# MLP up-projection of a two-layer decoder trunk: twelve gate column pairs computed from seven block products each

## The chip, the cores and the metric

One core of one Trainium2 chip runs the whole kernel. The metric is the device time of one execution in microseconds (us), lower is better. The engines are called as the profile calls them: PE is the matrix engine (TensorE) and PEld its weight load, DVE the vector engine, ACT the scalar engine, POOL GpSimd, and SP the engine whose queue issues the loads. SBUF is the on-chip working memory, PSUM the memory of eight banks (128 partitions by 512 float32 each) that PE writes its results to.

## What is computed

Two layers over 512 tokens with a width of 1024. Each layer has a mixer (attention with a short convolution in layer 0, gated linear attention in layer 1), then a gated MLP, then an embedding added through a gate. The change lies in the MLP:

```python
def _conv_ffn(h, w_up, conv_w, conv_b, w_down):
    u = _causal_depthwise_conv(h @ w_up, conv_w) + conv_b
    gate, up = jnp.split(u, 2, axis=-1)
    return (jax.nn.gelu(gate, approximate=False) * up) @ w_down

# in each layer:
x = x + _conv_ffn(_rms_norm(x, ffn_norm[i]), ffn_w_up[i], ffn_conv_w[i], ffn_conv_b[i], ffn_w_down[i])
```

`w_up` is 1024 by 5632: 2816 gate columns and 2816 value columns. The convolution runs over three tokens of each column by itself. `_rms_norm` divides a token by the root mean square of its 1024 values and multiplies by a gain.

## The kernel before

All large products are made in float32 from two parts: an operand is split into a high part (a cast to the reduced float `fp32r`, made on ACT) and a low part (the difference, made on DVE), and `mm3` (L153) issues three matmuls, high by high, high by low, low by high. `split` (L96) does this for activations, `cut` (L118) for weights.

**The up-projection** is `ffn` (L770). Activations lie transposed, 128 features by 512 tokens, in eight tiles `xT`. `xg` holds them times the gain and split, as eight pairs in the buffers with the tags a0 and a1, eight of each; the division by the root mean square is not in them. It comes later, as a multiplication by `R` (a tile with each token's factor), in `taps`. The loop over d = 0 to 10, called blocks here, takes 256 gate columns and the 256 value columns that belong to them. A block loads two weight tiles of 1 MB into `raw` (two buffers, SP queue), cuts each into two pairs `wh`, `wl` (three buffers of each), and then computes four columns of 128: gate and value for c = 0, gate and value for c = 1. A column is 8 x 3 = 24 matmuls of 512 tokens that gather in one PSUM bank from `ps` (four banks; `pa` has the other four).

For each column, `taps` multiplies the bank by R into `z` (DVE, L785), scales it and adds the bias (ACT, L786) and adds the two earlier tokens with two fused multiply-adds (DVE, L788). The gate goes through Gelu (ACT, L810), gate and value are multiplied (DVE, L813), and the product is split at once (L101, L102) into its place in `acts`: the first eight of 22 in the buffers b0 and b1, the others in quarters of tiles tagged `four` (seven buffers). `zt`, the tile of tap results, has four buffers of 512 columns.

After the loop, `project` (L349) multiplies `acts` with the down-projection's weights, two output columns at a time, eight products of gate and value (k) at a time, and `done` adds the result to `xT`. In layer 1, `blocks` (L281) there prepares sums of halves for `ple1`, the last stage, which already works from seven products of quarter matrices.

**Order.** Within `manual_schedule` blocks the named engines keep the program's order. Elsewhere the framework's planner sets the order of each engine's instructions when the kernel is built, from estimated costs, the program's order and when buffers come free. Engines run their queues in that order. Two instructions on different engines that touch the same PSUM bank are kept apart.

Of the kernel before, what the change touches and what calls it, by code (L numbers as in the profile page):

```python
# [18 lines left out]
P = 128  # L19
S = 512  # L20
D = 1024
NT = S // P
ND = D // P
DFF = 2816
NF = DFF // P
# [31 lines left out]
class Kernel:  # L57
# [709 lines left out]
            self.end_norm()  # L767


    def ffn(self, i, next_gain):  # L770
        nc, a, tc = self.nc, self.a, self.tc
        xg, R = self.xg, None
        wu = a["ffn_w_up"][i].rearrange("(k p) n -> p k n", p=P)
        w0, w1, w2, bb = self.fcv
        with tc.tile_pool(name=f"ffn{i}", bufs=1) as fp:
            acts = [self.pair(self.fp, "b0", "b1") for f in range(8)]
            for f in range(8, NF, 2):
                four = self.four(fp)
                acts += [(four[:, 0], four[:, 1]), (four[:, 2], four[:, 3])]

            def taps(ps, f):
                y = fp.tile([P, S], F32, tag="zt", name=self.nm("zt"), bufs=4)
                z = fp.tile([P, S + 2], F32, tag="z", name=self.nm("z"), bufs=3)
                nc.gpsimd.memset(z[:, :2], 0.0)
                nc.vector.tensor_tensor(z[:, 2:], ps, R, ALU.mult)  # L785
                nc.scalar.activation(y, z[:, 2:], AF.Identity, scale=w2[:, f : f + 1], bias=bb[:, f : f + 1])  # L786
                for tap, w in ((1, w1), (0, w0)):
                    nc.vector.scalar_tensor_tensor(  # L788
                        out=y, in0=z[:, tap : tap + S], scalar=w[:, f : f + 1], in1=y, op0=ALU.mult, op1=ALU.add
                    )  # L790
                return y

            for d in range(NF // 2):
                wg = self.weights(wu[:, :, 256 * d : 256 * d + 256], ND, 256)
                wv = self.weights(wu[:, :, DFF + 256 * d : DFF + 256 * d + 256], ND, 256)
                for c in range(2):
                    f = 2 * d + c
                    got = []
                    pss = []
                    for w in (wg, wv):  # L800
                        ps = self.ps()
                        for k in range(ND):
                            self.mm3(ps, w(k, c * P, (c + 1) * P), xg[k], start=k == 0, stop=k == ND - 1)
                        pss.append(ps)
                    if R is None:
                        R = self.spread()
                    for w, ps, fo in ((wg, pss[0], f), (wv, pss[1], NF + f)):
                        y = taps(ps, fo)
                        if w is wg:
                            nc.scalar.activation(y, y, AF.Gelu)  # L810
                        got.append(y)
                    g, y = got
                    nc.vector.tensor_tensor(y, g, y, ALU.mult)  # L813
                    self.split(acts[f], y)
            self.begin_norm(("a0", "a1"))
            done = self.residual(next_gain)
            if i == 1:
                self.forms = []
                scratch = lambda: fp.tile([P, S], F32, tag="zt", name=self.nm("gx"), bufs=4)

                def done(m, ps):
                    nc.vector.tensor_tensor(self.xT[m], self.xT[m], ps, ALU.add)
                    self.blocks(m, next_gain, scratch)
# [75 lines left out]
    def ple1(self, fp):  # L899
# [49 lines left out]
        def back(hf, t):  # L949

            pb = self.pa()
            for q in range(4):
                nc.tensor.transpose(
                    pb[:, q * P : (q + 1) * P], self.xT[4 * hf + q][:, t * P : (t + 1) * P], self.ident
                )
            x = fp.tile([P, 512], F32, tag="zt", name=self.nm("xt"), bufs=4)
            nc.scalar.copy(x, pb)
            return x

# [45 lines left out]
        X, Q = [[self.ps() for _ in range(2)] for _ in range(2)]  # L1005
        both = (0, H)
        with tc.manual_schedule(engines={ET.PE, ET.DVE, ET.Activation}):
# [3 lines left out]
            steps = [(j, i, both, Q[i]) for j in range(J) for i in range(2)]  # L1011
# [38 lines left out]
            halves = ((0, H // 2), (H // 2, H))  # L1050
# [482 lines left out]
```

## Time and profile before

| | |
|---|---|
| runs of the kernel before | 1247.49, 1248.13, 1248.69 us; median 1248.13 |
| the profiled execution | 1248.2 us, of it 1246.4 us span from the first to the last instruction |
| clock granted to PE in it | 1.000 |
| bytes moved by DMA | 117.45 MB, mean 94 GB/s |
| up-projection, layer 0 | about 186 to 425 us of the span |
| up-projection, layer 1 | about 828 to 1068 us of the span |

How to read it: a row of the groups names line, engine, operation, output <- inputs, shape and count, then busy us, mean ns of one, and the idle time of the engine just before, with what ended it. A matmul's row gives its length with the drain, which overlaps the next; the spacing of starts in the timeline is what one costs. Fences in the prediction show whole lines of the views, with "..." where lines are left out.

### The profile page before, as it was taken

The numbers are of one execution on the slowest core, as the hardware profiler recorded it, in microseconds if no ns is written. First come the engines' busy times: TensorE is split into PE (matmuls) and PEld (weight loads), VectorE is DVE, ScalarE is ACT, GpSimd is POOL, SyncE is SP. The second block draws the span as 40 slices with busy tenths as digits, with TensorE's granted clock in tenths as the row PEclk, the third lists the DMA queues.
The fourth block names the chain that finished last, engine by engine and source line by source line (L and its number), as shares of the span: only waits on it lengthen the run. The fifth ranks groups of instructions, "written<-read, shape, count | busy, mean of one in ns | idle before, by whom it ended". The sixth has DMA issues, their size and how long they took to land.

```text
span 1246.4 us, 15216 instructions
## 1 busy us (share of the span) xinstructions
PE 1236.1 (99%) x5984; PEld 1023.9 (82%) x5984; DVE 804.6 (65%) x1251; ACT 561.5 (45%) x873; POOL 52.1 (4%) x152
## 2 busy tenths in 40 slices
PE   9999999999999999999999999999999999999998
PEld 8877788888888888888987878888888888888887
DVE  6886556777777633346679875557777777444495
ACT  7466344444444322234563554335444444333374
POOL 2500000000000000000100000000000000000000
PEclk9999999999999999999999999999999999999999
DMA  6222232233333232223322222332223333322411
GB/s 214 92 80 56 83 102 83 88 100 102 101 102 101 83 103 93 93 74 103 111 91 68 69 68 68 101 110 95 83 94 102 101 101 102 101 93 94 149 46 68
DMA packets 111004, 117.45 MB, mean 94 GB/s; under 512 B 2728, under 2 KB 106210, under 8 KB 110932
## 3 DMA queue, kind: packets, MB, share of 16 engines
q1 hardware_dynamic: 109568, 115.35, 28.4%
q8 instruction: 47, 0.77, 0.2%
q0 software_dynamic: 560, 0.42, 0.2%
q10 hardware_dynamic: 804, 0.70, 0.2%
q14 instruction: 25, 0.20, 0.0%
HBM read 114.37 MB, written 2.10 MB: 93 GB/s over the span
## 4 chain that ended last, share of the span: by engine, by line
PE 88%; DVE 7%; ACT 2%; issue 1%; POOL 1%; DVEq 0%; ACTq 0%; POOLq 0%
PE ps L157 26%; PE ps L158 26%; PE ps L159 26%; DVE wl L138 1%; PE ps L947 1%; PE ps L946 1%; PE ps L945 1%; PE pa L1367 1%; PE pa L1344 0%; PE pa L595 0%; PE pa L158 0%; PE pa L192 0%; PE pa L159 0%; DVE F L1228 0%; PE pa L157 0%
## 5 line engine op out<-in xcount | busy, mean ns | idle before, releaser
L137 ACT ACTIVATE wh<-raw 128x1024 fp32r<-128x1024 f32 (+4 forms) x212 | 214.2, 1012 | 333.3 <-PE ps L158 298.7
L138 DVE TENSOR_TENSOR wl<-raw,wh 128x1024 fp32r<-128x1024 f32 (+4 forms) x212 | 246.5, 1164 | 153.2 <-ACT wh L137 152.1
L157 PE MATMUL ps<-a,wh 128*128 128x512 f32 x864 | 336.9, 390 | 0.0
L158 PE MATMUL ps<-a,wh 128*128 128x512 f32 x864 | 336.6, 390 | 0.0
L159 PE MATMUL ps<-a,wl 128*128 128x512 f32 x864 | 336.3, 389 | 0.0
L158 PEld LDWEIGHTS ps<-a,wh 128*128 128x128 f32 x864 | 162.3, 188 | 34.0 <-issue 0.3
L159 PEld LDWEIGHTS ps<-a,wl 128*128 128x128 f32 x864 | 162.2, 188 | 33.9
L157 PEld LDWEIGHTS ps<-a,wh 128*128 128x128 f32 x864 | 162.2, 188 | 33.7 <-issue 0.7
L788 DVE SCALAR_TENSOR_TENSOR zt<-z,vfa,zt 128x512 f32<-128x512 f32 x176 | 131.3, 749 | 3.6 <-ACT zt L786 0.6
L157 PE MATMUL ps<-b,wh 128*128 128x512 f32 x320 | 126.0, 395 | 0.5 <-ACT b L101 0.5
L159 PE MATMUL ps<-b,wl 128*128 128x512 f32 x320 | 125.7, 393 | 0.0
L158 PE MATMUL ps<-b,wh 128*128 128x512 f32 x320 | 125.0, 391 | 0.0
L785 DVE TENSOR_TENSOR z<-ps,R 128x512 f32<-128x512 f32 x88 | 60.3, 687 | 74.7 <-PE ps L159 74.7
L157 PE MATMUL ps<-four,wh 128*128 128x512 f32 x224 | 87.1, 389 | 0.0
L158 PE MATMUL ps<-four,wh 128*128 128x512 f32 x224 | 87.1, 389 | 0.0
L159 PE MATMUL ps<-four,wl 128*128 128x512 f32 x224 | 87.1, 389 | 0.0
L786 ACT ACTIVATE zt<-z,vfb 128x512 f32<-128x512 f32 x88 | 70.9, 808 | 5.0 <-DVE z L785 3.3
L157 PEld LDWEIGHTS ps<-b,wh 128*128 128x128 f32 x320 | 60.0, 188 | 14.0 <-ACT b L101 1.3
L159 PEld LDWEIGHTS ps<-b,wl 128*128 128x128 f32 x320 | 60.1, 188 | 12.5
L158 PEld LDWEIGHTS ps<-b,wh 128*128 128x128 f32 x320 | 60.1, 188 | 12.5
L810 ACT ACTIVATE zt<-zt 128x512 f32<-128x512 f32 x44 | 27.8, 631 | 74.9 <-DVE zt L788 74.8
L101 ACT ACTIVATE four<-zt 128x512 fp32r<-128x512 f32 x28 | 17.7, 632 | 77.3 <-DVE zt L813 77.3
(359 smaller groups left out, 1555.0 us busy)
## 6 DMA issues: line engine op xcount, KB each, us to landing
raw<-in_ffn_w_up_dram SPq DMA_DIRECT2D x44, 1024.0 KB, 5.1
raw<-in_ffn_w_down_dram SPq DMA_DIRECT2D x16, 1024.0 KB, 4.7
raw<-in_hy_w_in_dram SPq DMA_DIRECT2D x8, 1024.0 KB, 5.0
raw<-in_gla_w_in_dram SPq DMA_DIRECT2D x8, 1024.0 KB, 5.3
raw<-in_ffn_w_down_dram SPq DMA_DIRECT2D x8, 768.0 KB, 4.1
raw<-in_ple_w_gate_dram SPq DMA_DIRECT2D x6, 1024.0 KB, 4.7
raw<-in_gla_w_out_dram SPq DMA_DIRECT2D x4, 1024.0 KB, 4.8
raw<-in_gla_w_in_dram SPq DMA_DIRECT2D x4, 672.0 KB, 4.0
```

Source lines behind the costliest of these rows:

```text
L101: nc.scalar.activation(h, src, AF.Copy)
L137: nc.scalar.activation(hv, v, AF.Copy)
L138: nc.vector.tensor_tensor(lv, v, hv.bitcast(F32), ALU.subtract)
L157: mm(out, lh, rh, start=start, stop=False)
L158: mm(out, lh, rl, start=False, stop=False)
L159: mm(out, ll, rh, start=False, stop=stop)
L785: nc.vector.tensor_tensor(z[:, 2:], ps, R, ALU.mult)
L786: nc.scalar.activation(y, z[:, 2:], AF.Identity, scale=w2[:, f : f + 1], bias=bb[:, f : f + 1])
L788: nc.vector.scalar_tensor_tensor(out=y, in0=z[:, tap : tap + S], scalar=w[:, f : f + 1], in1=y, op0=ALU.mult, op1=ALU.add)
L810: nc.scalar.activation(y, y, AF.Gelu)
L945: mm(o, lh, rh, start=first and j == 0, stop=False, **kw)
L946: mm(o, lh, rl, start=False, stop=False, **kw)
```

## The change

For blocks d = 4 to 9 of each layer (`SEVEN`), the two gate columns are computed in another way. Input features, gate columns and tokens are each split in two, which makes the product of two gate columns a product of matrices of 2 by 2 quarters. Instead of eight quarter products, seven are computed (a Strassen-like form), each with 4 x 3 matmuls of 256 tokens. `sums` makes the four sums of token quarters (once a layer, in blocks 0 to 3, as splits in b0 and b1), `seven_forms` the sums of weight quarters, and `seven` issues the products. `W` and `V` are banks of `pa`; `X` and `Y` (banks of `ps`) hold the two results, with 256 tokens in each half. Copies on ACT seed and pass on partial sums; `more`, the product V, is added to `Y` in `taps`. The first value column of a block, `V0`, is computed in two halves between the products, the second, `V1`, behind them (before them in block 4). PE's order is kept by hand in these blocks.

The sums have to be formed from normed activations, so from block 4 on x times gain times R is the operand: `sums` computes it into `scratch`, and at block 4 it is split into eight new a0, a1 pairs. From there `taps` no longer multiplies by R and reads PSUM directly. Products of gate and value stay in float32 in `kept` (tiles tagged `four`), since b0 and b1 are in use; all 22 are split after block 9, the first eight one by one, the others two at a time. `zt` has two buffers of 1024 columns, so that Gelu and the product run over both columns at once. The memsets of two columns of `z` on POOL are gone. In the last stage `half()` hands out halves of the `zt` tiles.

```diff
+SEVEN = (4, 10)
+    def sums(self, j, gain, R, scratch):
...
+        for u in range(2):
+            m = 2 * j + u
+            nc.vector.scalar_tensor_tensor(
+                out=scratch[:, u], in0=self.xT[m], scalar=gain[:, m : m + 1], in1=R, op0=ALU.mult, op1=ALU.mult
+            )
+        e, o, s12, s34 = (scratch[:, u] for u in range(4))
+        out = []
+        nc.vector.tensor_tensor(s12[:, :H], e[:, H:], o[:, H:], ALU.add)
...
+        for x in (s12, s34):
+            hl = self.pair(self.fp, "b0", "b1")
+            self.split(hl, x)
...
+    def seven_forms(self, raw):
...
+        (b11, b12), (b21, b22) = self.blocks_of(raw)
+        plain = self.cut_blocks(raw[:, :, :P])
+        nc.vector.tensor_tensor(b11, b12, b11, ALU.subtract)
+        nc.vector.tensor_tensor(b12, b22, b12, ALU.subtract)
+        t13 = self.cut_blocks(raw.rearrange("p (j u) n -> p j u n", u=2)[:, :, 0])
+        nc.vector.tensor_tensor(b11, b22, b11, ALU.subtract)
+        t2 = self.cut_blocks(b11, False)
+        nc.vector.tensor_tensor(b21, b21, b11, ALU.subtract)
+        return plain, t13, t2
+
+    def seven(self, raw, ws, xg, forms):
...
+        W, V = self.pa(), self.pa()[:, :H]
+        X, Y = self.ps(), self.ps()
...
+        def product(out, w, c, x, first=False):
...
+            for j in range(ND // 2):
+                (wh, wl), (xh, xl) = w(j, c), x(j)
+                mm(out, wh, xh, start=first and j == 0, stop=False, **kw)
+                mm(out, wh, xl, start=False, stop=False, **kw)
+                mm(out, wl, xh, start=False, stop=j == ND // 2 - 1, **kw)
...
+        product(W[:, left], plain, 0, tokens(0, 0), True)
+        nc.scalar.copy(X[:, left], W[:, left])
+        nc.scalar.copy(Y[:, left], W[:, left])
+        product(V, t13, 0, s1, True)
+        more = self.sp.tile([P, S], F32, tag="acc", name=self.nm("more"), bufs=1)[:, :H]
+        nc.scalar.copy(more, V)
+        product(X[:, left], plain, 1, tokens(1, 0))
+        product(Y[:, left], t2, 0, s2)
+        nc.scalar.copy(X[:, right], Y[:, left])
+        yield
+        last = self.cut_blocks(raw.rearrange("p (j u) n -> p j u n", u=2)[:, :, 1])
+        product(X[:, right], t13, 1, s3)
+        nc.scalar.copy(Y[:, right], X[:, right])
+        yield
+        product(Y[:, left], last, 1, s4)
+        product(X[:, right], last, 0, tokens(1, 1))
+        yield X, Y, more
...
     def ffn(self, i, next_gain):
...
+            scratch = [self.four(fp, F32) for _ in range(ND // 2)]
             for d in range(NF // 2):
-                wg = self.weights(wu[:, :, 256 * d : 256 * d + 256], ND, 256)
-                wv = self.weights(wu[:, :, DFF + 256 * d : DFF + 256 * d + 256], ND, 256)
...
-                    self.split(acts[f], y)
+                g, y = both(), both()
+                normed = d >= SEVEN[0]
+                if d == SEVEN[0]:
+                    xg = []
+                    for m in range(ND):
+                        xg.append(self.pair(self.fp, "a0", "a1"))
+                        self.split(xg[m], scratch[m // 2][:, m % 2])
...
+                    with tc.manual_schedule(engines={ET.PE}):
+                        if d == SEVEN[0]:
+                            rg, rv = loaded(d)
+                            V1 = second()
+                            taps(y[:, 1], V1, NF + 2 * d + 1)
+                            ws, w = self.seven_forms(rg), column(rv, 0)
+                        steps = self.seven(rg, ws, xg, forms)
+                        next(steps)
+                        V0 = self.pa()
+                        value(w, V0, 0, ND // 2)
+                        next(steps)
+                        value(w, V0, ND // 2, ND)
+                        X, Y, more = next(steps)
+                        if d > SEVEN[0]:
+                            V1 = second()
+                        if d + 1 < SEVEN[1]:
+                            rg, rv = loaded(d + 1)
+                            ws, w = self.seven_forms(rg), column(rv, 0)
+                        taps(y[:, 0], V0, NF + 2 * d)
+                        taps(g[:, 0], X, 2 * d)
+                        taps(g[:, 1], Y, 2 * d + 1, more)
+                        nc.scalar.activation(g, g, AF.Gelu)
+                        if d > SEVEN[0]:
+                            taps(y[:, 1], V1, NF + 2 * d + 1)
+                else:
...
+                nc.vector.tensor_tensor(u, g, y, ALU.mult)
+                if d < ND // 2:
+                    forms.append(self.sums(d, gain, R, scratch[d]))
+                if d == SEVEN[1] - 1:
+                    for f in range(8):
+                        hl = self.pair(self.fp, "b0", "b1")
+                        self.split(hl, at(f))
+                        acts.append(hl)
+            for d in range(4, NF // 2):
+                split_pair(y if d == NF // 2 - 1 else kept[d // 2][:, 2 * (d % 2) : 2 * (d % 2) + 2])
```

`cut_blocks` casts 1024 weights a partition (512 for t2, in the buffers tagged `sq`) into one pair `wh`, `wl` and returns its quarters; `column` cuts one value column of 1024; `loaded` issues the two loads of a block.

More of the change, by code (lines that the diff above doesn't have):

```diff
@@ L793, in ffn @@
-            for d in range(NF // 2):
-                wg = self.weights(wu[:, :, 256 * d : 256 * d + 256], ND, 256)
-                wv = self.weights(wu[:, :, DFF + 256 * d : DFF + 256 * d + 256], ND, 256)
[L796 to L813, printed above, removed]
-                    self.split(acts[f], y)
+            forms, kept, acts = [], [], []
@@ new lines, in columns, with loaded, column @@
+            def columns(w, c, bank):
+                ps = bank()
+                for k in range(ND):
+                    self.mm3(ps, w(k, c * P, (c + 1) * P), xg[k], start=k == 0, stop=k == ND - 1)
+                return ps
+            def loaded(d):
+                out = [self.raw(ND, 256) for _ in range(2)]
+                for raw, c0 in zip(out, (256 * d, DFF + 256 * d)):
+                    nc.sync.dma_start(raw, wu[:, :, c0 : c0 + 256])
+                return out
+            def column(raw, c):
+                return self.cut(raw[:, :, c * P : (c + 1) * P], "b")
```

112 lines of the change are left out of this document (95 added, 17 removed).

## The prediction

> **What bounds the kernel now.** I read the engines' busy times first, then who the matrix engine (PE) waited for, then the chain that ended last.
>
> ```profile
> PE 1236.1 (99%) x5984; PEld 1023.9 (82%) x5984; DVE 804.6 (65%) x1251; ACT 561.5 (45%) x873; POOL 52.1 (4%) x152
> ...
> PE 88%; DVE 7%; ACT 2%; issue 1%; POOL 1%; DVEq 0%; ACTq 0%; POOLq 0%
> ```
> ```profile
> PE pa L1213 <- DVE F L1211: 1.5, 2, 1.0
> PE pa L1287 <- ACT qT L1279: 1.3, 2, 0.7
> ...
> PE ps L157 <- ACT b L101: 0.5, 1, 0.5
> ```
>
> PE is busy 99% of the span, the chain is 88% PE, and its waits come to some 6 us in all, none of them in the stage that is changed. So time is saved here by fewer PE microseconds or not at all, and whatever makes PE wait is paid in full. Next the stage itself: blocks d = 4 to 9 (the ones that change) of layer 0 and of layer 1, in the view of windows (columns: us, then busy us and instruction count of PE, weight load, DVE, ACT, POOL; clock, DMA share, GB/s).
>
> ```profile
> 272.80:403.30 130.50, 130.50 (x577) 108.09 (x576) 95.47 (x120) 58.92 (x72) 2.39 (x24) 1.00 0.30 97
> 915.50:1046.00 130.50, 130.50 (x577) 108.07 (x576) 95.46 (x120) 58.89 (x72) 2.39 (x24) 1.00 0.30 97
> ```
>
> Six blocks take 130.5 us: 21.75 us each, PE full, DVE 15.9 us (73%), ACT 9.8 us (45%), clock 1.00. A block is 4 columns of 24 matmuls. Two starts of the same place in the pattern, 48 matmuls apart, in the timeline of PE:
>
> ```profile
> 272.78 0.39 PE L157 MATMUL ps<-a,wh 128*128 128x512 f32 x1
> ...
> 283.66 0.39 PE L157 MATMUL ps<-a,wh 128*128 128x512 f32 x1
> ```
>
> (283.66 - 272.78) / 48 = 0.2267 us from start to start for 512 columns; the 0.39 is the length of one with its drain, which overlaps the next.
>
> **What the change removes on PE.** In twelve blocks (six in each layer) the two gate columns, 48 matmuls of 512 columns, become seven products of 12 matmuls, 84 of 256 columns. The price of a 256-column matmul stands in the trace twice, in the last 24 matmuls of the kernel and, in 29 in a row, near its start:
>
> ```profile
> 1239.30 0.28 PE L945 MATMUL ps<-wh,a 128*128 128x256 f32 x1
> ...
> 1242.06 0.28 PE L947 MATMUL ps<-four,b 128*128 128x256 f32 x1
> ```
> ```profile
> 19.75 0.28 PE L158 MATMUL pa<-wl,a 128*128 128x256 f32 x1
> ...
> 23.11 0.28 PE L159 MATMUL pa<-wh,a 128*128 128x256 f32 x1
> ```
>
> 2.76 / 23 and 3.36 / 28 are both 0.120 us, more than half of 0.2267: each matmul carries about 0.013 us that doesn't shrink. So seven eighths of the arithmetic do not give an eighth back: gates before 48 x 0.2267 = 10.88 us, after 84 x 0.120 = 10.08 us. The two value columns stay at 10.88. A block goes from 21.76 to 20.96 us, 0.80 us less, **9.6 us over twelve blocks**. That is all the change can win; nothing else leaves PE. A rule that speaks against it is in the Trainium skill, "TensorE: Matmul & The Clock Gate", section "Back-to-back issue gap": it gives 81 ns for 128 and 131 ns for 512 columns in a stream with weight loads; a straight line between gives an estimate of 98 ns for 256, by which the gates would go from 6.3 to 8.2 us. The trace disagrees with it at 512 columns (227 ns).
>
> **What it adds beside PE.** Durations of the stage, from the groups by shape within the window of blocks 4 to 9, and from other lines a 256-column copy on ACT, a 256-column sum on DVE, the hand-over from PE to ACT and the landing time of a load:
>
> ```profile
> L158 PEld LDWEIGHTS ps<-a,wh 128*128 128x128 f32 x192 | 36.0, 188 | 7.5
> ...
> L788 DVE SCALAR_TENSOR_TENSOR zt<-z,vfa,zt 128x512 f32<-128x512 f32 x48 | 35.9, 749 | 0.8
> L138 DVE TENSOR_TENSOR wl<-raw,wh 128x1024 fp32r<-128x1024 f32 x24 | 29.4, 1225 | 3.0 <-ACT wh L137 2.7
> L137 ACT ACTIVATE wh<-raw 128x1024 fp32r<-128x1024 f32 x24 | 25.5, 1062 | 15.4 <-PE ps L158 15.4
> L786 ACT ACTIVATE zt<-z,vfb 128x512 f32<-128x512 f32 x24 | 19.4, 809 | 0.5
> L785 DVE TENSOR_TENSOR z<-ps,R 128x512 f32<-128x512 f32 x24 | 16.5, 687 | 22.4 <-PE ps L159 22.4
> L813 DVE TENSOR_TENSOR zt<-zt,zt 128x512 f32<-128x512 f32 x12 | 8.3, 692 | 0.4
> L102 DVE TENSOR_TENSOR four<-zt,four 128x512 fp32r<-128x512 f32 x11 | 7.6, 692 | 7.7 <-ACT four L101 7.7
> ...
> L101 ACT ACTIVATE four<-zt 128x512 fp32r<-128x512 f32 x11 | 7.0, 632 | 30.4 <-DVE zt L813 30.4
> ```
> ```profile
> L1351 ACT COPY st<-pa 128x256 f32<-128x256 f32 x4 | 1.5, 375 | 0.0
> ```
> ```profile
> L303 DVE TENSOR_TENSOR gx<-gx,gx 128x256 f32<-128x256 f32 x4 | 1.7, 420 | 0.2 <-ACT gx L288 0.2
> ```
> ```profile
> 1242.37 0.47 ACT L989 ACTIVATE so<-ps,rtok 128x256 f32<-128x256 f32 x1 [0.96 <-PE ps L947]
> ```
> ```profile
> raw<-in_ffn_w_up_dram SPq DMA_DIRECT2D x44, 1024.0 KB, 5.1
> ```
>
> DVE in a block of the seven: five low halves of 1024 (plain, t13, last, two value columns) 5 x 1.22 = 6.1; four weight differences and t2's low half, 5 x 0.69 = 3.5; eight taps 6.0; the sum with `more` 0.69; the product of gate and value in one go, priced as another 128x1024, 1.22. The four multiplications by R and both splits are gone from the block. Sum 17.5 us; the same counting of the old block gives 16.4 where the window shows 15.9 (neighbours overlap a little), so I take 17.0 of 20.96 us, 81%. ACT: casts 5 x 1.06 + 0.63, four scalings 3.2, Gelu about 1.06, five copies of 256 columns 1.9: 12.1 us, 58%. Both stay under PE. Blocks 0 to 3 lose a split (1.4) and gain the token sums (two fused multiplications 1.5, four halves 1.7, two splits 1.4): DVE some 19 of 21.75 us; they depend on nothing of the block and have the whole layer's four blocks to be done in. POOL's memsets go; nobody on the chain waited for them. Bytes moved stay the same, on the same SP queue.
>
> **Where PE could wait inside a block.** Count t from the block's first matmul: products 1 to 4 end at 1.44, 2.88, 4.32, 5.76, the value half at 8.48, product 5 at 9.92, the other half at 12.64, products 6 and 7 at 15.52, the second value column at 20.96. The copies: ACT began 0.03 us after PE's last result above (1242.06 + 0.28 against 1242.37), so the copy of W into X runs from 1.63 to 2.0 and is wanted at 2.88; the copies into the right halves have 2.72 us of value matmuls over them. Cost nothing, cover 0.85 us at the tightest, and 0.2 us each time that a 1.06 us cast stands right in front. The weights: three buffers for five uses. `last` is cut after product 3 and gives the raw buffer back at about 8; the next gate load takes 5.1 us and lands at 13; plain, two differences and t13 are then 1.06 + 1.22 + 0.69 + 0.69 + 1.06 + 1.22, with the hand-overs done at about 19.2, wanted at 22.4. The next value column's buffer comes free at 20.96, it is cut by 23.3, wanted at 26.7. So each chain has some 3.3 us of slack while 6.7 us of taps compete for DVE. I take 0, since the planner that orders DVE and ACT sees those chains first in the program; the other end is 1.9 us a block (below).
>
> **The switch at block 4.** This is the term I am least sure of. The normed x is split into the eight a0/a1 buffers that block 3's last column is still reading: buffer k comes free 24 - 3(k + 1) matmuls before its end, and block 4's first column wants the new pair k 0.68 k us after it. A split takes 0.63 on ACT and 0.69 on DVE, so alone it would be ahead by about 3 us. But DVE has in the same stretch block 3's last taps (0.69 + 1.5, twice), its product 1.22, the cut of the first value column 1.22, and after it plain, t13 and the differences. If the splits go first, 0. If all earlier work goes first, I count 2.9 us until pair 7, 0.5 for plain and 2.2 for t13: 5.6. I take 2.0 a layer, nearer to the low end because plain's buffer is free 10.9 us earlier; **4.0 us for both**.
>
> **The end of the stage.** The splits of all 22 products of gate and value move behind block 9: 8 x 0.69 for the first eight and 7 x 1.22 for the rest, two at a time, 14.1 us of DVE. Block 9 makes no forms for a successor (7 us less) and block 10 needs 12 of its 21.76 us, which leaves some 20 us of room, and the down-projection's first 48 matmuls (10.9 us) read only eight columns. Cost 0; without that cover what is left over would be paid.
>
> **Sum.** From the profiled execution's 1248.2 (span 1246.4): 1248.2 - 9.6 + 4.0 = 1242.6; the runs' median is 0.07 lower, so **1242.5**, its own range 1238.5 (switch free) to 1245.6.
>
> **Rivals.** (1) DVE sets the pace, and the change is slower. Its order is fixed in advance, and in the old block it is idle 21.75 - 15.9 = 5.85 us behind ACT and PE. If the new block keeps that idleness, it lasts 17.0 + 5.85 = 22.85 us: 1.9 us over PE's 20.96, 22.7 us over twelve, 1265; half of it gives 1254. For it: five casts in place of four in the ACT-to-DVE relay, the in-place differences that wait for both halves of t13. Against: much of the old idleness was waiting for PE columns (22.4 us of the window behind L785), which is slack, not need. It decides from 0.47 us of wait a block, (9.6 - 4.0) / 12. (2) The switch costs its upper end: 11.2 - 9.6, 1249.8, no change that can be told (0.2%, 2.5 us, is what a measurement of this kernel can tell). For it: blocks 3 and 4 together ask DVE for about all its time. Against: the splits are ready before the work that competes. (3) The weight load of 188 ns doesn't hide behind a 256-column matmul when every one has new weights: 84 x 0.188 = 15.8, a block 4.9 us longer, 59 us, 1307. Against it: all the 0.120 us matmuls above had their own loads. The Trainium skill's section named above gives its own version of this, an estimate of 1.9 us a block or 1271.
>
> **How the numbers follow.** Forecast 0.60, (1) 0.25, (2) 0.12, (3) 0.03. Faster by over 0.2% is the forecast, 0.60. Within: (2) and the mildest part of (1), 0.13. Slower: the rest of (1) and (3), 0.27. The range runs from 1238, PE's full gain, to 1262; beyond it lie the worst third of (1), (3), and a little below, some 0.15 together.
>
> **What would show it.** Matmuls of 256 columns at 0.120 us start to start, 36 x 12 = 432 more matmuls, and PE busy about 9.6 us less are the gain. The first pairs of block 4 (a0/a1 splits) among what PE waited for, some 2 us in each layer, would be the switch. Waits of PE for wl, wh or a copy that recur with each of the twelve blocks would be rival 1. The forecast is wrong if blocks 5 to 9 take over 21.4 us each, if the 256-column matmuls keep another spacing, or if the first columns of the down-projection wait for b0/b1 splits.

## The result, and the profile after

The changed kernel takes 1258.03 us (median of 6 runs, 1257.71 to 1259.87) against 1247.78 us for the kernel before (6 runs, 1247.06 to 1248.69): a ratio of 1.0084, 95% interval 1.0071 to 1.0097. It is 10.25 us slower where 5.6 us of gain were forecast, and the time lies within the predicted range but on the other side of no change. The profile is that of the execution of 1259.87 us (span 1258.1), 11.7 us above the profiled one of the kernel before.

The page of the changed kernel, engines' busy times and the chain that ended last:

```profile
PE 1235.7 (98%) x6416; PEld 1039.1 (83%) x6416; DVE 850.1 (68%) x1323; ACT 601.2 (48%) x963; POOL 43.6 (3%) x64
...
PE 81%; DVE 12%; ACT 4%; issue 2%; POOL 1%; DMA 0%; ACTq 0%; DVEq 0%; POOLq 0%
```

PE has the 432 more matmuls and is hardly less busy than the 1236.1 us of before; the chain has lost 7 points of PE to DVE and ACT. So PE waited, and some of its work got longer. Windows of the changed kernel, blocks 2 to 5 of layer 0 (us, then busy us and counts of PE, weight load, DVE, ACT, POOL; clock, DMA share, GB/s):

```profile
229.10:250.90 21.80, 21.80 (x98) 18.02 (x97) 15.18 (x18) 8.79 (x12) 0.00 (x0) 1.00 0.38 124
250.90:272.65 21.75, 21.75 (x97) 18.02 (x96) 21.29 (x34) 12.86 (x19) 0.00 (x0) 1.00 0.21 69
272.65:300.71 28.06, 24.16 (x134) 20.41 (x132) 20.65 (x28) 11.70 (x19) 0.00 (x0) 0.94 0.23 76
300.71:321.74 21.03, 21.03 (x135) 19.09 (x134) 17.82 (x23) 11.54 (x17) 0.00 (x0) 1.00 0.30 101
```

Block 5 is the forecast block: 21.03 us where 20.96 was worked out, PE full. Block 4, the one with the switch, takes 28.06 us, has PE idle for 3.9 of them and a mean clock of 0.94. In block 3 just before it DVE is busy for 21.29 of 21.75 us (the prediction said some 19), while block 2 leaves it 6.6 us. What PE waited for, in the changed kernel (us in all, times, longest):

```profile
PE pa L842 <- ACT wh L807: 3.4, 2, 1.7
PE ps L842 <- ACT ps L853: 2.8, 5, 0.7
PE pa L159 <- DVE a L103: 2.6, 6, 0.8
PE pa L844 <- DVE wl L808: 1.9, 4, 0.8
...
PE ps L158 <- ACT wh L138: 0.9, 2, 0.5
```

Of these the first, third and fourth lie in block 4 (casts and low halves of t13's and plain's weights, splits of the normed x), the second is the copy into X ahead of product 3 in five of the later blocks, the last is block 10. The timeline of PE in block 4 shows the longest of them and what came after it:

```profile
279.70 0.50 PE L159 MATMUL pa<-a,wh 128*128 128x512 f32 x1 [0.76 <-DVE a L103]
...
282.00 0.28 PE L844 MATMUL pa<-a,wl 128*128 128x256 f32 x1
283.97 0.38 PE L842 MATMUL pa<-b,wh 128*128 128x256 f32 x1 [1.69 <-ACT wh L807]
...
285.23 0.39 PE L844 MATMUL pa<-b,wl 128*128 128x256 f32 x1 [0.76 <-DVE wl L808]
...
287.04 0.41 PE L844 MATMUL ps<-a,wl 128*128 128x256 f32 x1
287.25 0.41 PE L842 MATMUL ps<-a,wh 128*128 128x256 f32 x1
287.46 0.41 PE L843 MATMUL ps<-a,wh 128*128 128x256 f32 x1
```

The last three start 0.21 us apart where 0.120 is the price. A window over that stretch gives the cause, a granted clock of 0.53:

```profile
286.30:289.90 3.60, 3.60 (x20) 3.60 (x19) 2.00 (x4) 1.60 (x3) 0.00 (x0) 0.53 0.66 220
```

Adding up, over all matmuls of the up-projection, what lies between two starts beyond 226.67 ns (512 columns) or 120 ns (256) gives 10.9 us for layer 0 and 9.9 us for layer 1, against 0.1 each in the kernel before. Of it 7.0 us a layer are the switch and 0.85 a layer block 10; the five copies are 4.1 in all, and 0.9 in all is the value columns, some of whose matmuls start a little further apart. (These figures hold the 0.1 us or so by which the matmul after a waiting one is late too.) Less the forecast gain of 9.6 us, the stage has to be 11.0 us longer, and it is: from its first matmul to the first of the down-projection 246.82 and 245.82 us, against 240.84 and 240.80 before. That is 11.0 of the 11.7 us between the two profiled executions. The other 0.7 us lies outside the stage, and the median of the runs loses 1.4 us less than the profiled execution; I didn't follow either. The question is why the operands were late.

The DVE timeline of the changed kernel at the switch shows a queue without a pause (start, duration):

```profile
277.22 0.69 DVE L103 TENSOR_TENSOR a<-four,a 128x512 fp32r<-128x512 f32 x1
277.82 1.22 DVE L991 TENSOR_TENSOR four<-zt,zt 128x1024 f32<-128x1024 f32 x1
278.96 0.69 DVE L103 TENSOR_TENSOR a<-four,a 128x512 fp32r<-128x512 f32 x1
279.56 1.22 DVE L808 TENSOR_TENSOR wl<-raw,wh 128x1024 fp32r<-128x1024 f32 x1
280.82 0.69 DVE L819 TENSOR_TENSOR raw<-raw 128x512 f32<-128x512 f32 x1
281.43 0.74 DVE L895 SCALAR_TENSOR_TENSOR zt<-pa,vfa,zt 128x511 f32<-128x511 f32 x1
282.09 0.68 DVE L820 TENSOR_TENSOR raw<-raw 128x512 f32<-128x512 f32 x1
```

The splits that PE wants (L103) take turns with block 3's taps, and block 3's product of gate and value (L991) stands ahead of the last one. Its result is wanted only when block 9 is done, more than 100 us later; what waits for it sooner is the first scaling of block 4 (L893 on ACT), since the product frees the `zt` buffers, and that scaling can wait: in e10 it began at 282.78 without a wait of PE. The difference L820 ends at 282.77, t13's cast follows on ACT, and PE has t13 at 283.97. Two theories fit this: A, DVE has time enough if the free time of block 2 is used, and its order makes the waits; B, DVE (81% busy by the forecast, 98% in block 3) has too much work there whatever the order.

### The profile page after: what moved, and what is told of

The parts are those of the page before. It is cut to its first block, busy times and chain, and to the rows that moved or that the text cites. A ratio compares the mean times of both kernels' runs of the same rounds, so it can differ in the third digit from the quotient of the medians.

```text
span 1258.1 us, 16088 instructions
## 1 busy us (share of the span) xinstructions
PE 1235.7 (98%) x6416; PEld 1039.1 (83%) x6416; DVE 850.1 (68%) x1323; ACT 601.2 (48%) x963; POOL 43.6 (3%) x64
## 4 chain that ended last, share of the span: by engine, by line
PE 81%; DVE 12%; ACT 4%; issue 2%; POOL 1%; DMA 0%; ACTq 0%; DVEq 0%; POOLq 0%
PE ps L158 18%; PE ps L159 18%; PE ps L160 18%; PE pa L159 4%; PE pa L158 3%; PE pa L160 3%; PE ps L842 2%; PE ps L843 2%; PE ps L844 2%; DVE wl L139 2%; DVE zt L895 1%; PE ps L1141 1%; PE ps L1140 1%; PE ps L1139 1%; ACT wh L138 1%
## 5 line engine op out<-in xcount | busy, mean ns | idle before, releaser
L138 ACT ACTIVATE wh<-raw 128x1024 fp32r<-128x1024 f32 (+4 forms) x188 | 188.5, 1006 | 365.8 <-PE ps L159 294.1
L139 DVE TENSOR_TENSOR wl<-raw,wh 128x1024 fp32r<-128x1024 f32 (+4 forms) x188 | 217.1, 1156 | 180.7 <-ACT wh L138 180.7
L158 PE MATMUL ps<-a,wh 128*128 128x512 f32 x480 | 187.8, 391 | 0.9 <-ACT wh L138 0.9
L159 PE MATMUL ps<-a,wh 128*128 128x512 f32 x480 | 187.3, 390 | 0.0
L160 PE MATMUL ps<-a,wl 128*128 128x512 f32 x480 | 186.5, 390 | 0.0
L158 PEld LDWEIGHTS ps<-a,wh 128*128 128x128 f32 x480 | 90.2, 188 | 20.6 <-ACT wh L138 1.8
L160 PEld LDWEIGHTS ps<-a,wl 128*128 128x128 f32 x480 | 90.1, 188 | 19.3 <-DVE wl L139 0.5
L159 PEld LDWEIGHTS ps<-a,wh 128*128 128x128 f32 x480 | 90.2, 188 | 18.8 <-issue 0.3
L159 PE MATMUL pa<-a,wh 128*128 128x512 f32 x192 | 75.8, 395 | 2.6 <-DVE a L103 2.6
L158 PE MATMUL pa<-a,wh 128*128 128x512 f32 x192 | 75.2, 391 | 0.0
L160 PE MATMUL pa<-a,wl 128*128 128x512 f32 x192 | 74.8, 389 | 0.0
L895 DVE SCALAR_TENSOR_TENSOR zt<-z,vfa,zt 128x511 f32<-128x511 f32 (+1 forms) x88 | 65.3, 747 | 3.8 <-ACT zt L893 3.2
L808 DVE TENSOR_TENSOR wl<-raw,wh 128x1024 fp32r<-128x1024 f32 x36 | 44.0, 1221 | 21.0 <-ACT wh L807 17.7
```

Of the source, the lines that this page charges most:

```text
L138: nc.scalar.activation(hv, v, AF.Copy)
L139: nc.vector.tensor_tensor(lv, v, hv.bitcast(F32), ALU.subtract)
L158: mm(out, lh, rh, start=start, stop=False)
L159: mm(out, lh, rl, start=False, stop=False)
L160: mm(out, ll, rh, start=False, stop=stop)
L808: nc.vector.tensor_tensor(l, src, h.bitcast(F32), ALU.subtract)
```

## Experiments

Ten runs, each against runs of the kernel before on the same chip (their medians 1247.78 to 1247.99 us). The expectations of e1 to e7 call it theory D that DVE is late at block 4, which A and B share; their rivals B, S and P are named in each.

| run | median us | ratio to before, 95% |
|---|---|---|
| e1_sums_early | 1272.07 | 1.0191 (1.0174 to 1.0208) |
| e2_plain_gates | 1252.75 | 1.0037 (1.0024 to 1.0050) |
| e3_copy_cover | 1254.73 | 1.0054 (1.0039 to 1.0069) |
| e4_fill | 1255.48 | 1.0061 (1.0046 to 1.0076) |
| e6_sums_pool | 1272.38 | 1.0198 (1.0181 to 1.0215) |
| e7_pool_cover | 1270.83 | 1.0181 (1.0163 to 1.0198) |
| e8_switch_order | 1248.23 | 1.0003 (0.9994 to 1.0012) |
| e9_all_order | 1247.40 | 0.9996 (0.9987 to 1.0005) |
| e10_value_first | 1240.63 | 0.9938 (0.9924 to 0.9952) |
| e11_order_plain | 1249.13 | 1.0009 (1.0000 to 1.0018) |

### e1: the token sums earlier

```diff
-                if d < ND // 2:
-                    forms.append(self.sums(d, gain, R, scratch[d]))
+                if d < ND // 4:
+                    for j in (2 * d, 2 * d + 1):
+                        forms.append(self.sums(j, gain, R, scratch[j]))
```

> The token sums of all four pairs are made in blocks 0 and 1 (two pairs in each) and none in blocks 2 and 3; nothing else differs from the changed kernel. Theory D (DVE is late at block 4: the sums of the last two pairs, about 9 us of DVE, stand in block 3 and push the new a0/a1 splits, the first weight forms and t13 behind what PE wants): PE's waits in block 4 for a0/a1 pairs and for t13 go from 5.5 us a layer to under 2, the clock stays at full in block 4, block 4 goes from 27.4 us to 21 to 23 us, and the kernel from 1258 to 1247 (1245 to 1251). Rival B (the old a0/a1 buffers come free too late, whatever DVE does): the waits for a0/a1 pairs stay above 1.5 us a layer, 1256 to 1258. Rival S (the loss sits in the seven products themselves, in copies between banks): within 1 us of 1258.

It took 14 us more than the change. The waits for splits in block 4 went, t13's stayed (1.58 and 1.13 us), and a new wait came in block 2, on PE's and then on DVE's timeline of this run:

```profile
238.03 0.80 PE L160 MATMUL ps<-a,wl 128*128 128x512 f32 x1 [6.50 <-DVE wl L139]
```
```profile
236.09 0.42 DVE L785 TENSOR_TENSOR four<-four 128x256 f32<-128x256 f32 x1
236.42 0.42 DVE L784 TENSOR_TENSOR four<-four 128x256 f32<-128x256 f32 x1
236.76 1.22 DVE L139 TENSOR_TENSOR wl<-raw,wh 128x1024 fp32r<-128x1024 f32 x1
```

Block 2's weights (L139) stand behind the half sums (L783 to L786), which nothing needs for over 40 us. The sums come earlier in the program than the next block's weights, and the planner put them first. Here it is the order that makes the wait; but the experiment also moved work from later blocks into blocks 1 and 2, so it didn't yet tell A from B.

### e2: ordinary gates behind the same switch

```diff
-                if SEVEN[0] <= d < SEVEN[1]:
+                if False:
```

> Blocks 4 to 9 compute their gates as ordinary columns of 512 tokens, with the normed operand; the sums, the new a0/a1 splits at block 4 and the late splits of the products stay. No seven products, no weight forms, no copies between banks. Theory D: the switch still costs, though less, since 7 us of weight forms are gone from DVE around block 4: 1 to 4 us a layer, 1250 to 1255. Rival B: 2 us a layer and more at the a0/a1 pairs, 1252. Rival S: nothing is lost, 1247 to 1249.

1252.75 us, 4.9 over the kernel before without one product of seven in it. The excess by the spacing of starts is 1.9 us in each layer, all of it at the switch (splits 0.95 us, a low half 0.57 us, and the late matmuls behind them), the clock is 1.00. So the move to a normed operand costs by itself 3.8 us of the 4.9, about what was forecast for the whole switch; where the last 1 us lies I didn't follow. The rest of the changed kernel's 7.0 us a layer comes with the seven products, whose weight forms are wanted at the same moment, and with the clock.

### e3: a product between the copy and its reader

The matmuls of V0 are issued in three pieces, behind products two, four and five.

```diff
         nc.scalar.copy(more, V)
+        yield
...
-                        value(w, V0, 0, ND // 2)
+                        value(w, V0, 0, 2)
+                        next(steps)
+                        value(w, V0, 2, 5)
                         next(steps)
-                        value(w, V0, ND // 2, ND)
+                        value(w, V0, 5, ND)
```

> The first value column is cut into three pieces in place of two: 2 of its 8 k behind product 2 (new cover for the copies into X and Y), 3 behind product 4, 3 behind product 5. Theory D: only the waits of product 3 for the copy into X go (2.8 us in five blocks, some 3.6 us with the slow start behind each), the switch stays: 1254 to 1255. Rival S (the copies are the main loss): 1248 or less. If the value weights are late for their earlier place, a new wait of about 0.5 us a block takes the gain back: 1258 and more.

3.3 us faster than the change, and no wait for L853's copy is left. In the changed kernel the copy is late because ACT has four other instructions first; its timeline in block 6, and PE's:

```profile
321.76 1.06 ACT L138 ACTIVATE wh<-raw 128x1024 fp32r<-128x1024 f32 x1 [1.25 <-PE pa L159]
322.72 0.76 ACT L893 ACTIVATE zt<-pa,vfb 128x512 f32<-128x512 f32 x1
323.38 1.05 ACT L975 ACTIVATE zt<-zt 128x1024 f32<-128x1024 f32 x1
324.33 0.62 ACT L807 ACTIVATE t<-raw 128x512 fp32r<-128x512 f32 x1
324.85 0.37 ACT L853 COPY ps<-pa 128x256 f32<-128x256 f32 x1
```
```profile
325.28 0.39 PE L842 MATMUL ps<-a,wh 128*128 128x256 f32 x1 [0.51 <-ACT ps L853]
```

ACT is 55% busy over block 5 (11.54 of 21.03 us), and yet in block 6 the copy starts some 1.4 us after product 1's last result (block 6 starts at 321.74, twelve matmuls and a drain later is 323.4).

### e4: the wait for t13 filled with matmuls

Ahead of product 2 of block 4, 15 matmuls of 256 columns multiply ones by ones into V, which product 2 then overwrites.

```diff
+        if fill:
+            ones = self.ones_r.unsqueeze(1).to_broadcast([P, 2, P])
+            for _ in range(fill):
+                mm(V, self.ones_r, ones, start=True, stop=True)
...
-                        steps = self.seven(rg, ws, xg, forms)
+                        steps = self.seven(rg, ws, xg, forms, 15 if d == SEVEN[0] else 0)
```

> In block 4 of each layer PE runs 15 matmuls of 256 columns with ones (1.8 us) into bank V before product 2, where it now waits 1.85 us for t13; their result is overwritten by the product. Theory D with the clock as its second part (after the waits of block 4 PE runs at a lower granted clock, 0.213 us for a 256-column matmul in place of 0.120, over 15 to 20 matmuls, 1.4 to 1.9 us a layer): the matmuls fill the wait, the clock stays up or falls for less long, 1254.5 to 1257. Rival (the slow spacing behind the wait has to do with the products or their operands and not with PE's idleness): the spacing of 0.213 stays, 1258 or a little more.

2.55 us faster than the change though PE does more. The same stretch as above, in this run:

```profile
286.30:289.90 3.60, 3.56 (x28) 3.31 (x28) 2.75 (x4) 2.13 (x4) 0.00 (x0) 1.00 0.72 221
```

Clock 1.00 and 28 matmuls in place of 20. The waits for L103 and L808 stayed as they were (2.6 and 1.9 us), those for L853's copy are four in place of five (2.0 us for 2.8). The two stages take 244.63 and 244.61 us for 246.82 and 245.82; less the 1.0 of the copy in layer 0 that is 1.2 us a layer, and half of the 2.55 is 1.3. So 1.2 to 1.3 us of each layer's loss was the clock that drops behind the wait for t13, and the drop goes when that one wait is filled.

### e6 and e7: the sums on POOL

The scaling goes to ACT, the multiplication by R and the four half sums to POOL; e7 adds the edit of e3 and, in block 10, PE in the program's order.

```diff
-            nc.vector.scalar_tensor_tensor(
-                out=scratch[:, u], in0=self.xT[m], scalar=gain[:, m : m + 1], in1=R, op0=ALU.mult, op1=ALU.mult
-            )
+            nc.scalar.activation(scratch[:, u], self.xT[m], AF.Copy, scale=gain[:, m : m + 1])
+            nc.gpsimd.tensor_tensor(scratch[:, u], scratch[:, u], R, ALU.mult)
...
-        nc.vector.tensor_tensor(s12[:, :H], e[:, H:], o[:, H:], ALU.add)
+        nc.gpsimd.tensor_tensor(s12[:, :H], e[:, H:], o[:, H:], ALU.add)
```

> The token sums stay in blocks 0 to 3 but leave DVE: ACT scales by the gain, POOL multiplies by R and makes the four half sums; DVE keeps only their two splits (1.4 us a block in place of 4.6). Nothing is reordered by hand. Theory D, amount (DVE has more work around block 4 than time, whichever order it has): DVE is ahead by 3 to 6 us at block 4, the waits for a0/a1 pairs and for t13 shrink from 5.5 to under 2.5 us a layer, the clock stays up: 1248 to 1252. Theory D, order (the planner's order alone puts t13's chain behind block 3's product and the splits): the waits for t13 stay as they are (2.7 us a layer) and only those for the pairs go: 1252 to 1256. Rival P: POOL and DVE share a way to SBUF, DVE's instructions get longer in blocks 0 to 3 and nothing is won: 1257 to 1262.

> The sums on POOL, the value column in three pieces (2, 3 and 3 of its 8 k behind products 2, 4 and 5), and PE's order in block 10 kept as the program has it. Theory D: the three savings add up (6 to 10 us, 3.3 us, 1.7 us): 1243 to 1247, not slower than before. Rival P or D, order: 1249 to 1255.

Both are 13 to 14 us slower than the change. Groups of e6 on POOL, groups of DVE in a stretch in which POOL ran all the time (258 to 264 us), and the waits:

```profile
L779 POOL TENSOR_TENSOR four<-four,R 128x512 f32<-128x512 f32 x16 | 32.1, 2012 | 105.7 <-ACT four L778 105.7
```
```profile
L894 DVE SCALAR_TENSOR_TENSOR zt<-z,vfa,zt 128x511 f32<-128x511 f32 x1 | 1.8, 1775 | 0.0
L139 DVE TENSOR_TENSOR wl<-raw,wh 128x1024 fp32r<-128x1024 f32 x1 | 1.7, 1720 | 0.0
```
```profile
ACT b L102 <- POOL four L783: 32.1, 8, 4.5
```

POOL takes 2.0 us for a multiplication of 128x512, DVE's instructions with both inputs in SBUF run 1.4 to 2.4 times as long beside it (1.78 against 0.74 us, 1.72 against 1.22), and ACT's splits wait at the head of its queue for POOL's results, up to 4.5 us with the casts of weights behind them. The work off DVE did not help, and since two things got worse at once this run doesn't price theory B. In e7 the waits for the copies were gone again; its order for block 10 made a wait of 1.46 us where 0.63 had been.

### e8: the same instructions in the order in which PE wants them

Nothing is added or left out. `seven_forms` becomes a generator with a stop behind the first four forms.

```diff
+                    for j in {1: (0, 1), 2: (2,), 3: (3,)}.get(d, ()):
+                        forms.append(self.sums(j, gain, R, scratch[j]))
+                    if d == SEVEN[0] - 1:
+                        rg, rv = loaded(d + 1)
+                        first = column(rv, 1)
                     for c in range(2):
                         pss = [columns(w, c, self.ps) for w in (wg, wv)]
...
+                        if d == SEVEN[0] - 1 and c == 1:
+                            xg = []
+                            for m in range(ND):
+                                xg.append(self.pair(self.fp, "a0", "a1"))
+                                self.split(xg[m], scratch[m // 2][:, m % 2])
+                            made = self.seven_forms(rg)
+                            next(made)
                         taps(g[:, c], pss[0], 2 * d + c, None, normed)
...
-                if d < ND // 2:
-                    forms.append(self.sums(d, gain, R, scratch[d]))
...
```

> The sums of the eight pairs (L778 to L784) are issued behind the weights of blocks 1 (two pairs), 2 and 3 in place of ahead of some of them; block 4's loads, the forms of its first value column, the splits of the eight summed tiles and the first four weight forms of its products are issued behind block 3's last weights and ahead of block 3's last taps, so that VectorE works in the order in which TensorE wants the operands. Nothing is added or left out. Theory A (VectorE has enough time in blocks 1 to 4, and its order makes the waits of block 4): the waits of TensorE at the switch, 7.4 us a layer by the trace of the changed kernel with the matmuls at 213 ns among them, fall under 1.5 us a layer, the clock of block 4 stays at 1.00, the copies' and block 10's waits stay: 1258 - 2 x 6 to 7 = 1244 to 1246 us. Rival B (VectorE has too much work there whatever the order): the waits only move, into block 3 or to later forms, some 4 to 6 us a layer stay: 1252 to 1257 us.

1248.23 us: 9.8 faster than the change, 2 to 4 short of what A had forecast. The splits, plain and t13 cost nothing any more and the clock is 1.00. Left are 4.6 us in layer 0 and 5.5 in layer 1: the copies (0.67 us twice a layer), block 10 (0.63), later weight forms of blocks 4 and 5 (1.7 and 2.6 us), and 0.1 us or so behind each. The part of the weight forms moved, as B says, but it is less than half of what went.

### e9: copies and block 10 in order too

e8 with the edit of e3 in all blocks, and the splits of the first eight products of gate and value issued behind block 10's weights.

```diff
+                    if d == SEVEN[1]:
+                        for f in range(8):
+                            hl = self.pair(self.fp, "b0", "b1")
+                            self.split(hl, at(f))
+                            acts.append(hl)
...
```

> The order of e8_switch_order, and besides: the copy of the sixth product into X gets a step of its own and the first value column's matmuls are run in three pieces behind products two, four and five, so that a product lies between the copy and its reader; and the splits of the first eight activations (L102, L103) are issued behind block 10's weights in place of ahead of them. Theory A: e8's time less 3.3 us for the copies and 1 to 1.7 us for block 10: 1238.5 to 1242 us, which is the gain of the seven products (9.6 us) with under 4 us of waits left, faster than the 1247.9 us of the kernel before. Rival B (the waits only move): within 1 us of e8, or 1250 us and more.

1247.40 us, only 0.8 better than e8 and far from 1238.5 to 1242. All waits of e8 but one short one are gone, and a new one stands alone; PE's timeline and DVE's, and the clock just behind it:

```profile
280.53 0.40 PE L159 MATMUL pa<-a,wh 128*128 128x512 f32 x1
283.37 0.50 PE L160 MATMUL pa<-a,wl 128*128 128x512 f32 x1 [2.44 <-DVE wl L139]
```
```profile
280.36 1.22 DVE L1007 TENSOR_TENSOR four<-zt,zt 128x1024 f32<-128x1024 f32 x1
281.50 0.68 DVE L808 TENSOR_TENSOR t<-raw,t 128x512 fp32r<-128x512 f32 x1
282.10 1.22 DVE L139 TENSOR_TENSOR wl<-raw,wh 128x1024 fp32r<-128x1024 f32 x1
```
```profile
284.50:288.00 3.50, 3.50 (x19) 3.50 (x18) 0.39 (x2) 1.06 (x1) 0.00 (x0) 0.52 0.90 297
```

The edit of e3 moved the first piece of V0 ahead of product 3, and with it the moment when its weights are wanted, while DVE makes them behind those of product 4 (L808, `t2`) and behind block 3's product of gate and value (L1007). My expectation had left that out.

### e10: one exchange

```diff
-                            ws, w = next(made), column(rv, 0)
+                            w, ws = column(rv, 0), next(made)
```

> The kernel of e9_all_order with one exchange in block 4: the first value column's weights are cut (L138, L139) ahead of the last two weight differences (L823, L825) and their cast, since TensorE now wants that column 1.4 us before it wants those. Theory A: the one long wait that e9 kept (2.61 us a layer on the low half of that column, at 283.37 and 926.80 us, with 1.1 to 1.5 us of matmuls at 213 ns behind it) goes, nothing comes in its place: 1247.4 - 2 x 3.7 to 4.1 = 1239 to 1240.5 us, faster than the kernel before by 0.55 to 0.7 per cent. Rival B (VectorE has too much work at the switch): the wait moves to the last weight forms of the third product (up to 1.3 us a layer) or to block 5, and the time stays at 1243 us or above.

1240.63 us (1239.64 to 1240.67): 7.4 us or 0.62% faster than the kernel before, 17.4 faster than the change, just beyond the upper edge of what A expected (1239 to 1240.5). Page, windows of blocks 2 and 3 and of blocks 4 to 9 of layer 0, and DVE's timeline at the switch:

```profile
PE 1228.0 (99%) x6416; PEld 1036.4 (84%) x6416; DVE 849.4 (69%) x1323; ACT 602.4 (49%) x963; POOL 44.1 (4%) x64
```
```profile
229.00:250.80 21.80, 21.80 (x98) 18.03 (x97) 18.32 (x26) 10.28 (x14) 0.00 (x0) 1.00 0.38 123
250.80:272.55 21.75, 21.75 (x97) 18.02 (x96) 19.87 (x29) 12.51 (x18) 0.00 (x0) 1.00 0.22 71
272.55:399.12 126.57, 126.47 (x793) 114.53 (x792) 105.40 (x133) 75.24 (x111) 0.00 (x0) 1.00 0.31 100
```
```profile
269.93 0.69 DVE L819 TENSOR_TENSOR raw<-raw 128x512 f32<-128x512 f32 x1
270.53 4.30 DVE L103 TENSOR_TENSOR a<-four,a 128x512 fp32r<-128x512 f32 x7
274.75 0.68 DVE L820 TENSOR_TENSOR raw<-raw 128x512 f32<-128x512 f32 x1
...
279.12 1.23 DVE L139 TENSOR_TENSOR wl<-raw,wh 128x1024 fp32r<-128x1024 f32 x1
...
281.52 1.22 DVE L1007 TENSOR_TENSOR four<-zt,zt 128x1024 f32<-128x1024 f32 x1
```

All splits are done by 274.8 us, where the changed kernel made the last one at 279.65, and block 3's product of gate and value comes behind the first value column's weights. The new order also uses the time that DVE had free in block 2: 18.32 us of work there for 15.18, and 19.87 for 21.29 in block 3. DVE has the same 1323 instructions and 849.4 us of work, against 850.1 in the changed kernel. With the amount the same and 17.4 us gone, the order of the queues made the waits (PE's own included, which e3's edit changes): theory A. What B says holds for block 3 alone, and only in the old order. The six blocks take 126.57 us, 0.8 over the forecast six times 20.96.

### e11: the order without the seven products

e10 with ordinary gate columns in blocks 4 to 9; sums, splits and their order stay.

```diff
-                if SEVEN[0] <= d < SEVEN[1]:
+                if False:
...
-                    if d == SEVEN[0] - 1:
-                        rg, rv = loaded(d + 1)
-                        first = column(rv, 1)
...
-                            made = self.seven_forms(rg)
-                            next(made)
```

> The order of e10_value_first with the gates of blocks 4 to 9 in ordinary columns: the sums and their splits stay, with the order that e8 and e9 gave them, the seven products, their weight forms and copies are left out. It prices the seven products alone, with the switch in order in both kernels. Theory A (the products' gain of 576 matmuls of 512 columns at 226.67 ns less 1008 of 256 at 120 ns, 9.6 us, is real and was eaten by waits): 8 to 10 us above e10, 1247.5 to 1250 us. Rival C (the products themselves give less than the spacing says): under 6 us above e10.

1249.13 us, 8.5 above e10; blocks 4 to 9 of layer 0 in this run:

```profile
272.64:403.20 130.56, 130.56 (x578) 108.14 (x576) 82.18 (x94) 55.85 (x71) 0.00 (x0) 1.00 0.30 101
```

PE is full in both windows, 130.56 us here and 126.57 in e10: 4.0 us a layer by the trace. So the seven products are worth 8.0 to 8.5 us with nearly every operand in time, and the ordered switch costs PE nothing that the window shows: the six blocks take what they took in the kernel before.

## Why the prediction was wrong

**The gain on PE** was right: 0.120 us a matmul, block 5 in 21.03 us for 20.96. Measured alone it is 8.0 to 8.5 us of the 9.6. In e10 some 0.35 us a layer is waiting (in block 5, 21.4 us); most of the rest is value-column matmuls, about 95 a layer of which start 0.230 to 0.236 us apart in place of 0.227. I made no run on why.

**"The switch at block 4 ... I take 2.0 a layer"** is the step that failed, and it decides the sign. It is 28.06 - 20.96 = 7.1 us in layer 0 and about as much in layer 1, 14 us for the 4.0 in the sum. Both ends had been worked out, and the upper one, "if all earlier work goes first", 5.6, was nearly what happened: splits 1.8 us, plain 0.3, t13 1.85 + 0.9, together 4.9 us. I took the low end because plain's buffer is free early and left open in which order DVE would run, where the case turned on nothing else; and block 3, which I gave some 19 us of DVE, had 21.29 of its 21.75. And the upper end lacked a term: the half clock behind the wait, 1.2 to 1.3 us a layer (e4), and 0.1 us or so after each wait. e2, e8 and e10 bear the step out: 1.9 us a layer with the normed operand alone, nothing with the order put right.

**The copies, "Cost nothing, cover 0.85 us at the tightest, and 0.2 us each time that a 1.06 us cast stands right in front"**: five waits of 0.67 us and more, 4.1 us in all with what follows each, of which e3 got back 3.3. The mechanism was seen, its size was not: up to four instructions stand in front, not one.

**The end of the stage, "Cost 0"**: a wait of 0.63 us a layer in block 10, 0.85 with what follows it, where the splits issued in front of the weights made them late; gone in e9 and e10.

**Rival 1** (DVE sets the pace in every block) was the likeliest way to slower and is not what happened: blocks 5 and 9 ran at 21.0 us, block 5 with DVE at 17.82 us (17.0 forecast), and in e10 the six took 21.1 on average, with the same DVE work. Five of the ten blocks behind the switch did pass the 21.4 us named as a sign (21.8 to 22.0), but by the copies on ACT, not by DVE. **Rival 2** had the place right and, at 1249.8, the price too low, since it took the upper end without the clock, the copies and block 10. **Rival 3** fell: every 256-column matmul had its own weights at 0.120 us.

By the terms of the trace the sum is 1246.4 - 9.6 + 14.0 (twice 7.0) + 4.1 + 1.7 (twice 0.85) = 1256.6 of a span of 1258.1; of the 1.5 left, 0.9 is the spacing in the value columns and some 0.7 lies outside the stage. That the time fell inside the range is luck: the upper part of the range was there for rival 1, which didn't happen.

## What to carry to other kernels

Where a change saves little in each of many blocks and has one place where operands change over, price that place by the order in which the queues will really run, not by their share of busy time: DVE was 74% busy in block 4 (20.65 of 28.06 us) and still late, because work that PE didn't want yet stood in front, and because block 3 was full (98%) while block 2 left 6.6 us unused. When a planner goes by the program's order, issue the work in the order of its readers' needs; here that, with the same number of instructions on every engine, was worth 17.4 us. And after moving a reader earlier, look at once at what it reads: e9 lost 7 us to a single exchange.

## What the runs showed of the hardware

**The clock drops behind waits that are short, by what PE idled in one stretch of 3.41 us.** In the changed kernel no single wait of PE at the switch is over 1.85 us from the start that was due to the start that came, but behind them the granted clock is 0.5 for 3.41 us. In e9 one wait of 2.6 us does the same; in e4, with the longest wait filled, it stays at 1.00. Up to the end of the span, a drop lasts 3.41 us in all these traces (twice that in block 2 of e1), and the full clock between two drops of one run lasts whole multiples of it: 645.12 us, or 189 times 3.413, in the changed kernel, 51.2 us, or 15 times, in e1. So the clock goes by stretches of 3.413 us, which can be laid back from a drop. The one ahead of the drop in block 4, in the changed kernel:

```profile
283.01:286.42 3.41, 1.69 (x12) 1.49 (x13) 2.88 (x4) 1.86 (x2) 0.00 (x0) 1.00 0.00 0
```

PE idles for 1.72 us of it. In layer 1 of e3 the same waits fell into two stretches, with 1.34 and 1.29 us, and the clock stayed at 1.00. Over the twelve traces all 16 half-clock stretches ahead of the end of the span stand behind stretches with 1.52 us or more of idle PE, and only two stretches with over 1.5 us had none behind them (1.51 and 1.54). About 1.5 us idle of 3.41 is thus the limit that these runs show, and how a wait falls into the stretches is chance. That fits e9's eleven executions, of which one was traced: five had a mean clock of 0.999 or 1.000 and took 1245.9 to 1246.1 us, six had 0.997 or 0.998 and took 1247.4 to 1249.4. The Trainium skill, "TensorE: Matmul & The Clock Gate", section "Why this matters for your kernels", asks for no idle gaps of PE over about 3 us. The traces disagree: several shorter ones in one stretch are enough.

**POOL's elementwise work makes DVE slower.** 2.0 us for a multiplication of 128x512 on POOL, and 1.4 to 2.4 times their duration for DVE instructions with both inputs in SBUF that began while one ran (e6). In the same stretch a DVE instruction with one input in PSUM kept its 0.68 us (L891 at 259.81), and one with both in SBUF that began just before POOL's kept its 0.75 us (L894 at 222.49, POOL at 222.53). Those that began during an instruction of POOL ended 0.55 us (the taps, 0.74 long by themselves) or 1.1 us (those of 1.22) after its end, so they did most of their work behind it. The Trainium skill, "SBUF — State Buffer", section "SBUF: two separate sides", says that the two share a pair of ports as a lock and that the one that comes second is blocked. These traces agree.
